# Latent attention on row tiles: first keys, values and gate tiles placed between the first row maxima, the transposed scores regrouped, and the first output tile's split moved

## The chip, the core and the metric

The kernel runs on one core of one Trainium2 chip. The metric is device time in microseconds (us) of one execution. Before the change the median of 3 runs is 1684.32 us (1684.28 to 1687.16). The core's engines each have a queue of their own: PE (TensorE, matrix products into PSUM), ACT (ScalarE), DVE (VectorE), POOL (GpSimd) and SP (SyncE, which only issues transfers). PSUM has eight banks of 128 x 512 fp32.

## The reference

Two layers over 1024 latent tokens and 256 context tokens of width 1024, in fp32: layer 0 is windowed attention, layer 1 is latent attention, and a final RMSNorm follows. The change touches only layer 1's attention and its output projection:

```python
def attend(qn, qr, kn, kr, v):
    s = (jnp.einsum("bqhd,bkhd->bhqk", qn, kn)
         + jnp.einsum("bqhd,bkd->bhqk", qr, kr)).astype(F32) * scale
    p = jax.nn.softmax(s, axis=-1).astype(v.dtype)
    return jnp.einsum("bhqk,bkhd->bqhd", p, v)
...
yx = (ox * jax.nn.silu(gx)) @ w_out
...
x = x + gate_x[:, None] * yx
...
return rms_norm(x, final_g)
```

There are 16 heads with 64 + 32 query and key columns and 64 value columns. 1024 queries see 1280 keys. Queries, keys (from a rank-256 latent) and the gate `g` come from projections that run before.

## The kernel before

Layer 0, the projections of layer 1 and the query tiles run first, until about 1009 us. From line 1389 on the code stands in a block in which the order of the instructions on PE, ACT and DVE is written by hand; SP's and POOL's queues are ordered by the framework, which also lets a few matmuls of the second output tile slip in at the block's end.

**Precision.** Most products are made of two-part numbers (a rounded high part and the rest). `split` (lines 118 to 121) makes the parts: ACT copies the high part (L120), another engine subtracts (L121). `mm3` (L125 to L127) is high*high, low*high, high*low.

**Units.** Attention runs in 32 units: head pair `i // 4`, head `e` in the pair, half of 512 queries. One unit has these steps, written out of order around those of its neighbours:

- `prep` loads the queries by SP.
- `top(b)`, b = 0 to 3, finds a row maximum for 128 queries: four matmuls 64x512 (L1161, two at a time on the two halves of PE's rows) and two of 64x256 on one half (L1164) fill `psm` (banks 0 to 2), then DVE reduces 1280 columns to one (L1166). The next `top` writes the same banks, so it waits for that reduction.
- `shift` transposes the maxima (L1170, into a corner of bank 2), DVE spreads them (L1171), ACT copies them (L1176). They enter the scores as extra rows of the product.
- `score(i, a, b)`, i = 0 to 4, makes transposed scores, 256 keys by 512 queries, in passes a to b of five; a pass is a pair of matmuls (L1192), one on each half of the rows. Scores alternate between two pairs of banks, `slots`. `expo(i)` is the exponential on ACT (L1198) that empties the pair; POOL then adds up the denominators (L1202, L1206). `hold=True` leaves `expo` to be called later.
- `PV` multiplies with the values (L1214, 20 matmuls, bank 7), `fin` and `fin1` put the halves together (ACT L1229, DVE L1233), `fin2` and `fin3` transpose and apply denominators and gate (PE L1243 and L1258, DVE L1244, L1247, L1259, ACT L1252, POOL L1261) and store to `og_d`.

In the loop over `ui` (lines 1415 to 1472) unit `ui` has its scores made while unit `ui - 1` has its `PV` and `fin` steps, unit `ui + 2` its `top(0)` and `top(1)`, unit `ui + 1` its `top(2)`, `top(3)` and `shift`. `make_K` makes a pair's keys in two calls (with `ui % 4` 0 and 1), ACT casting (L1125) and DVE subtracting (L1123); `make_V` makes the values of four heads (`ui % 8 == 0`, L1098).

**Start.** Ahead of the loop stand the rotary keys (`make_kr`), the first keys and values, the last gate tiles (`g_tile`, 24 matmuls 128x256 a half, SiLU on ACT at L994) and the first unit's `top` calls. With the first unit's scores stand `top(1)` to `top(3)` of unit 1, `make_K(1, (0, 2))` and `top(0)`, `top(1)` of unit 2.

**Output.** `out_tiles` (line 1286) is a generator that handles eight tiles of 128 rows: fetch, split, 48 products for two banks of columns, gate and residual (L1346, L1347), squares (L1348), norm, store. For the first tile seven of eight column blocks are fetched early; block 7 needs unit 30's `fin3` to be stored first. `next(out_fill)` runs it to the next `yield`. `wo_pieces` splits the output weights in the same way.

Of the kernel before, what the change touches and what calls it, by code (L numbers as in the profile page):

```python
# [59 lines left out]
def kernel(ctx: ExitStack, tc: tile.TileContext, t, out, dbg=None):  # L60
    nc = tc.nc
# [979 lines left out]
    NU = 32  # L1041
# [7 lines left out]
    accr = Ring(F, [47, 49], 512)  # L1049
    glr = Ring(R, [60, 62], 512)  # L1050
    otr = Ring(F, [0, 4], 1024)
    rbr = Ring(F, [8, 9], 256)
# [6 lines left out]
    def slot():  # L1059
        slots.reverse()  # L1060
        return slots[1]
# [224 lines left out]
    def out_tiles():  # L1286
        load2(out=gx1, in_=gate_d[1, 0, :].partition_broadcast(128))

# [8 lines left out]
        yield  # L1297
        load(out=fg, in_=t["final_g"].partition_broadcast(128))
        for ti in range(8):
# [5 lines left out]
            n = 7 if ti == 0 else 8  # L1305
            split(og[:, 0, 0:n], og[:, 1, 0:n], of[:, 0:n])
            st = sm_ring()
            css = [slice(c * 512, c * 512 + 512) for c in range(2)]
# [80 lines left out]
    with tc.manual_schedule(engines={E.PE, E.Activation, E.DVE}):  # L1389
# [10 lines left out]
        g_tile(9, 3, 1)  # L1400
        next(vk)
        next(vk)
        u0.top(0)
        next(vk)
        u0.top(1)
        g_tile(8, 4, 0, slots[0][:, 0])
        g_tile(8, 4, 1)
# [3 lines left out]
        u0.top(3)  # L1411
        g_tile(9, 4, 1)
        u1.top(0)
        u0.shift()
        for ui, u in enumerate(units):
            pu, ppu = [units[ui - n] if ui >= n else None for n in (1, 2)]
            nu, nnu = [units[ui + n] if ui + n < NU else None for n in (1, 2)]
            if nnu and ui:
                nnu.prep()
            u.score(0, 0, 1)  # L1420
            if ui == 0:
                u.score(0, 1, 4)
                nu.top(1)
                u.score(0, 4, 5)
                u.score(1, 0, 3)
                nu.top(2)
                u.score(1, 3, 5, hold=True)
                nu.top(3)
            else:
                if nu:  # L1430
                    nu.top(2)
                u.score(0, 1, 5)
                u.score(1, 0, 4)
                if nu:
                    nu.top(3)
                u.score(1, 4, 5, hold=True)
            x = slot()
            if ui % 4 == 0 and u.pair < 7:
                make_K(u.pair + 1, (0, 2), x)
            if ui % 4 == 1 and u.pair < 7:  # L1440
                make_K(u.pair + 1, (1,), x)
            if ui == NU - 1:
                next(out_fill)
            if pu:
                pu.PV()
            u.expo(1)
            if ui % 4 > 1 and ui < 23 or ui > 25:
                next(wo_fill)
            if pu:
                pu.fin()  # L1450
            if nu:
                nu.shift()
            if ppu and ppu.e == 1:
                ppu.fin3(x[:, 0])
            if pu:
                pu.fin2(x[:, 1])
            if ui and ui % 8 == 0:
                pu.fin1()
                for _ in make_V(u.pair // 2, x):
                    pass  # L1460
            if ui == NU - 1:
                next(out_fill)
            if nnu:
                nnu.top(0)
            if ui % 8:
                pu.fin1()
            u.score(2)
            u.score(3, 0, 3)
            if nnu:
                nnu.top(1)  # L1470
            u.score(3, 3, 5)
            u.score(4)
# [6 lines left out]
        u.fin1()  # L1479
        next(out_fill)  # L1480
        u.fin2(slot()[:, 0])
        next(out_fill)
        u.fin3(slot()[:, 0])
# [75 lines left out]
```

## Time and profile before

| | us |
|---|---|
| profiled execution | 1683.97 |
| its span (first to last instruction) | 1682.1 |
| median of 3 runs | 1684.32 |
| PE busy | 1581.9 (94%) |
| DVE busy | 1023.7 (61%) |
| ACT busy | 796.9 (47%) |
| POOL busy | 802.0 (48%) |
| granted PE clock, mean | 0.977 |

The profile shows one execution; its times count from the span's start. PE's matmuls overlap, so a busy PE need not be PE at its peak; PEld is the load of a matmul's stationary operand. What stands in brackets at a row's end is the engine's idle time before that row and what ended it. Units 1 to 30 lie between 1081 and 1549 us, about 14.3 us each, 16.7 with a `make_K` and 23.5 with a `make_V`.

### The profile page before, as it was taken

Reading aid. Unit: us, or ns where it says so; the run is one execution under the profiler, and the core shown is the slowest. Engines: PE = TensorE matmul, PEld = TensorE weight load, DVE = VectorE, ACT = ScalarE, POOL = GpSimd, SP = SyncE. Lnnn points to the kernel's source line nnn. Section 1 sums busy time; section 2 is a strip of 40 time slices with the busy share of each in tenths; the row PEclk is TensorE's granted clock in tenths of the full one; section 3 lists DMA queues with packets and bytes.
Section 4 is the critical chain, followed back from the end, with each engine's and each line's share of the span. In section 5 each row is a group of like instructions: output and inputs, shape, how many; then the busy total and the mean of one; then the engine's idle time right before and its main releaser. Section 6 shows DMA issues by size and latency. Waiting matters only on the chain.

```text
span 1682.1 us, 26928 instructions
## 1 busy us (share of the span) xinstructions
PE 1581.9 (94%) x9738; PEld 1238.9 (74%) x9738; DVE 1023.7 (61%) x2047; ACT 796.9 (47%) x1541; POOL 802.0 (48%) x774
## 2 busy tenths in 40 slices
PE   6899739999999999998999999899999999999898
PEld 2787628888788888887998999566766666766587
DVE  7898773327888888878534102566566566566254
ACT  3621112237877777777423312454454544544321
POOL 2556552222544333344324410478677677678300
PEclk9999869999999999999999999999999999999899
DMA  8455565145433333326117632213233232233151
GB/s 308 140 169 166 147 175 163 50 150 161 118 107 101 92 88 88 89 63 219 38 51 236 223 112 73 66 36 93 62 91 93 68 90 77 64 122 100 55 171 65
DMA packets 145476, 192.68 MB, mean 115 GB/s; under 512 B 14256, under 2 KB 82480, under 8 KB 145344
## 3 DMA queue, kind: packets, MB, share of 16 engines
q1 hardware_dynamic: 143584, 188.41, 37.5%
q10 hardware_dynamic: 1760, 2.56, 0.5%
q8 instruction: 76, 1.25, 0.3%
q14 instruction: 56, 0.46, 0.1%
HBM read 144.77 MB, written 46.15 MB: 114 GB/s over the span
## 4 chain that ended last, share of the span: by engine, by line
PE 46%; DVE 3%; ACT 2%; issue 1%; DMA 1%; POOL 1%; ACTq 0%; POOLq 0%; DVEq 0%; SPq 0%
PE PB L1192 11%; PE PB L1214 8%; PE PB L125 7%; PE PB L127 7%; PE PB L126 7%; PE PB L1161 4%; ACT arena_f L1198 1%; PE PB L1164 1%; PE PB L1243 1%; DVE arena_f L1166 1%; PE PB L1170 0%; DVE arena_r L121 0%; DMA arena_f<-b_w_in 0%; DMA x_d<-arena_f 0%; PE PB L1258 0%
## 5 line engine op out<-in xcount | busy, mean ns | idle before, releaser
L125 PE MATMUL PB<-arena_r 128*128 128x512 f32 (+2 forms) x1496 | 511.5, 343 | 25.5 <-DVE arena_f L445 13.2
L126 PE MATMUL PB<-arena_r 128*128 128x512 f32 (+2 forms) x1496 | 506.7, 339 | 5.2 <-DVE arena_r L280 2.6
L127 PE MATMUL PB<-arena_r 128*128 128x512 f32 (+2 forms) x1496 | 504.1, 337 | 0.6 <-DVE arena_r L121 0.6
L1206 POOL TENSOR_TENSOR arena_f<-arena_f 128x512 f32<-128x512 f32 x252 | 328.7, 1304 | 127.3 <-ACT arena_f L1198 111.1
L125 PEld LDWEIGHTS PB<-arena_r 128*128 128x128 f32 x1496 | 287.0, 192 | 62.9 <-DVE arena_f L445 14.6
L126 PEld LDWEIGHTS PB<-arena_r 128*128 128x128 f32 x1496 | 287.4, 192 | 35.6 <-DVE arena_r L280 4.5
L127 PEld LDWEIGHTS PB<-arena_r 128*128 128x128 f32 x1496 | 287.0, 192 | 29.7 <-DVE arena_r L121 1.2
L1166 DVE TENSOR_REDUCE arena_f<-PB 128x1 f32<-128x1280 f32 x128 | 190.2, 1486 | 130.2 <-PE PB L1164 124.3
L1192 PE MATMUL PB<-arena_r 64*128 64x512 f32 (+1 forms) x1600 | 244.6, 398 | 2.0
L1198 ACT ACTIVATE arena_f<-PB 128x1024 f32<-128x1024 f32 x160 | 164.1, 1026 | 139.8 <-PE PB L1192 92.5
L121 POOL TENSOR_TENSOR arena_r<-arena_f,arena_r 128x512 fp32r<-128x512 f32 x98 | 139.2, 1435 | 183.7 <-ACT arena_r L120 139.2
L1192 PEld LDWEIGHTS PB<-arena_r 64*128 64x128 f32 (+1 forms) x1600 | 179.0, 186 | 40.6 <-ACT arena_f L1198 16.4
L552 DVE CUSTOM_DVE_ANT_0 arena_f<-PB,arena_f,small 128x256 f32<-128x256 f32 (+1 forms) x288 | 145.6, 522 | 28.1 <-PE PB L546 22.0
L121 DVE TENSOR_TENSOR arena_r<-PB,arena_r 128x512 fp32r<-128x512 f32 (+1 forms) x198 | 128.4, 657 | 27.6 <-ACT arena_r L120 27.0
L1214 PE MATMUL PB<-arena_f 128*64 128x512 f32 x640 | 144.4, 597 | 0.0
L194 DVE SCALAR_TENSOR_TENSOR arena_f<-arena_f,small 128x512 f32<-128x512 f32 x126 | 124.5, 1032 | 22.5 <-DMA arena_f<-ada_w 22.0
L555 ACT ACTIVATE arena_f<-arena_f,small 128x640 f32<-128x640 f32 (+2 forms) x160 | 119.3, 747 | 28.6 <-DVE small L554 27.8
L120 ACT CAST arena_r<-PB 128x512 fp32r<-128x512 f32 (+1 forms) x198 | 108.9, 561 | 49.3 <-PE PB L573 27.1
L583 PE MATMUL PB<-arena_r 128*128 128x512 f32 x336 | 123.3, 441 | 4.3 <-ACT arena_f L594 3.2
L120 ACT CAST arena_r<-arena_f 128x512 fp32r<-128x512 f32 (+2 forms) x146 | 87.1, 610 | 83.6 <-DVE arena_f L455 18.5
L573 PE MATMUL PB<-ident,arena_f 128*128 128x128 f32 x672 | 110.6, 274 | 1.3 <-ACT arena_f L555 1.1
L1214 PEld LDWEIGHTS PB<-arena_f 128*64 128x64 f32 x640 | 43.1, 137 | 81.4 <-issue 80.2
(157 smaller groups left out, 2082.0 us busy)
## 6 DMA issues: line engine op xcount, KB each, us to landing
arena_f<-ada_w SPq DMA_DIRECT2D x82, 256.0 KB, 3.6
arena_r<-q_d SPq DMA_DIRECT2D x80, 256.0 KB, 3.9
arena_r<-qn_d SPq DMA_DIRECT2D x64, 256.0 KB, 3.8
arena_r<-qr_d SPq DMA_DIRECT2D x192, 64.0 KB, 3.1
arena_f<-a_w_in SPq DMA_DIRECT2D x40, 256.0 KB, 3.2
q_d<-arena_f SPq DMA_DIRECT2D x80, 128.0 KB, 2.4
g_d<-arena_f SPq DMA_DIRECT2D x36, 256.0 KB, 2.9
arena_f<-x SPq DMA_DIRECT2D x16, 512.0 KB, 4.5
```

The source lines that it names most:

```text
L120: nc.scalar.copy(hi, src)
L121: (lo_eng or nc.vector).tensor_sub(lo, src, hi.bitcast(F32))
L125: nc.tensor.matmul(o, ah, bh, start=first, stop=False)
L126: nc.tensor.matmul(o, al, bh, start=False, stop=False)
L127: nc.tensor.matmul(o, ah, bl, start=False, stop=last)
L194: nc.vector.scalar_tensor_tensor(accs[i], w, sc[:, k, i : i + 1], accs[i], ALU.mult, ALU.add)
L552: nc.vector.tensor_tensor_reduce(o, S, mk, 1.0, prev, ALU.add, ALU.max, mx)
L1166: nc.vector.reduce_max(self.mx[:, 32 + b : 33 + b], flat, AX.X, negate=True)
L1192: nc.tensor.matmul(S[:, t], k[r, c : c + 128], q[r], start=j == 0, stop=j == 4)
L1198: nc.scalar.activation(E, self.S, AF.Exp)
L1206: eng.tensor_add(self.acc, self.acc, E[:, t])
L1214: nc.tensor.matmul(self.pv[p : p + 64], Vq[:, cs[t], self.h % 4, :], E[:, t], start=i == 0, stop=i == 4)
```

## The change

No product is added or dropped. One tiny activation is new (`warm`, one column through the exponential), and the load of the gate row `gx1` goes from ACT's queue to SP's. The rest is order:

```diff
 def out_tiles():
-    load2(out=gx1, in_=gate_d[1, 0, :].partition_broadcast(128))
+    load(out=gx1, in_=gate_d[1, 0, :].partition_broadcast(128))
...
     nxt = fetch(0, 7)
     yield
-    load(out=fg, in_=t["final_g"].partition_broadcast(128))
...
         split(og[:, 0, 0:n], og[:, 1, 0:n], of[:, 0:n])
+        if ti == 0:
+            yield
+            load(out=fg, in_=t["final_g"].partition_broadcast(128))
...
-    next(vk)
-    next(vk)
+    for _ in vk:
+        pass
     u0.top(0)
-    next(vk)
+    g_tile(8, 4, 0, slots[0][:, 0])
     u0.top(1)
-    g_tile(8, 4, 0, slots[0][:, 0])
     g_tile(8, 4, 1)
...
     g_tile(9, 4, 1)
+    nc.scalar.activation(warm, const[:, 1:2], AF.Exp)
+    u0.shift()
     u1.top(0)
-    u0.shift()
+    make_K(1, (0, 2), slots[1])
+    u1.top(1)
     for ui, u in enumerate(units):
...
-        u.score(0, 0, 1)
         if ui == 0:
-            u.score(0, 1, 4)
-            nu.top(1)
-            u.score(0, 4, 5)
+            u.score(0)
             u.score(1, 0, 3)
             nu.top(2)
             u.score(1, 3, 5, hold=True)
+            x = slot()
+            make_K(1, (1,), x)
             nu.top(3)
+            u.expo(1)
+            u.score(2)
+            nu.shift()
         else:
+            u.score(0, 0, 2)
             if nu:
                 nu.top(2)
-            u.score(0, 1, 5)
+            u.score(0, 2, 5)
...
+            if ui == NU - 2:
+                next(out_fill)
             pu.PV()
             u.expo(1)
...
+            if ui == NU - 1:
+                next(out_fill)
             pu.fin()
...
         if nnu:
             nnu.top(0)
...
-        u.score(2)
-        u.score(3, 0, 3)
+        if ui:
+            u.score(2)
+        u.score(3)
         if nnu:
             nnu.top(1)
-        u.score(3, 3, 5)
         u.score(4)
     pu.fin3(slot()[:, 0])
     next(out_fill)
     next(out_fill)
     u.PV()
     u.fin()
     u.fin1()
     next(out_fill)
+    next(out_fill)
     u.fin2(slot()[:, 0])
+    next(out_fill)
     next(out_fill)
     u.fin3(slot()[:, 0])
```

The `next(out_fill)` now at `NU - 2` stood at `NU - 1`, and the one now ahead of `pu.fin()` stood behind `pu.fin2`. Of the calls ahead of `PV` the loop's `make_K` lines stay, except that the call with block 1 for pair 1 is the one shown at `ui == 0`. The new lines move the numbers of the changed kernel's helper lines up by one: L1166 is L1167 there, and so on; in `out_tiles` by three.

PE in the loop, one unit before, from `fin2` (L1243) of the unit behind to `top(3)`: L1161 and L1164 are a `top`, L1192 the matmuls of `score`.

```order
L1243 MATMUL PB<-ident,arena_f 128x128 x4
L1161 MATMUL PB<-arena_r 128x512 x4
L1164 MATMUL PB<-arena_r 128x256 x2
L1192 MATMUL PB<-arena_r 128x512 x16
L1161 MATMUL PB<-arena_r 128x512 x4
L1164 MATMUL PB<-arena_r 128x256 x2
L1192 MATMUL PB<-arena_r 128x512 x16
L1161 MATMUL PB<-arena_r 128x512 x4
```

The same unit now:

```order
L1244 MATMUL PB<-ident,arena_f 128x128 x4
L1162 MATMUL PB<-arena_r 128x512 x4
L1165 MATMUL PB<-arena_r 128x256 x2
L1193 MATMUL PB<-arena_r 128x512 x20
L1162 MATMUL PB<-arena_r 128x512 x4
L1165 MATMUL PB<-arena_r 128x256 x2
L1193 MATMUL PB<-arena_r 128x512 x14
L1162 MATMUL PB<-arena_r 128x512 x4
```

Between `top(0)` and `top(1)` there were 16 matmuls and are 20; between `top(1)` and `top(2)`, and again between `top(2)` and `top(3)`, there were 16 and are 14.

DVE at the start, before: L1166 reduces for `top`, L1171 is `shift`, L1123 the subtractions of `make_K`.

```order
L1166 TENSOR_REDUCE arena_f<-PB 128x1 x5
L1171 TENSOR_TENSOR arena_r<-PB,ident 4x512
L1166 TENSOR_REDUCE arena_f<-PB 128x1 x3
L1123 TENSOR_TENSOR arena_r<-PB,arena_r 64x512 x2
L1123 TENSOR_TENSOR arena_r<-PB,arena_r 64x256 x4
L1171 TENSOR_TENSOR arena_r<-PB,ident 4x512
```

And now:

```order
L1167 TENSOR_REDUCE arena_f<-PB 128x1 x4
L1172 TENSOR_TENSOR arena_r<-PB,ident 4x512
L1167 TENSOR_REDUCE arena_f<-PB 128x1
L1124 TENSOR_TENSOR arena_r<-PB,arena_r 64x512 x2
L1124 TENSOR_TENSOR arena_r<-PB,arena_r 64x256 x4
L1167 TENSOR_REDUCE arena_f<-PB 128x1 x2
L1124 TENSOR_TENSOR arena_r<-PB,arena_r 64x512 x2
L1167 TENSOR_REDUCE arena_f<-PB 128x1
L1172 TENSOR_TENSOR arena_r<-PB,ident 4x512
```

The first unit's `shift` now stands ahead of unit 1's first reduction, and the six subtractions stand ahead of the reductions for unit 1's `top(1)` to `top(3)` where they stood behind them.

ACT in the last unit, before: L1198 is `expo`, L120 128x512 the split of a weight piece, L120 128x896 the split of the first output tile, L1229 `fin`, L1252 `fin2`.

```order
L1198 ACTIVATE arena_f<-PB 128x1024 x4
L1287 DMA arena_f<-gate_d 128x1024
L1198 ACTIVATE arena_f<-PB 128x1024
L120 CAST arena_r<-arena_f 128x512
L1229 COPY arena_f<-PB 64x512
L1252 COPY arena_f<-small 128x256 x2
L120 CAST arena_r<-arena_r 128x896
L1198 ACTIVATE arena_f<-PB 128x1024 x3
```

And now:

```order
L1199 ACTIVATE arena_f<-PB 128x1024 x5
L120 CAST arena_r<-arena_f 128x512
L120 CAST arena_r<-arena_r 128x896
L1230 COPY arena_f<-PB 64x512
L1253 COPY arena_f<-small 128x256 x2
L1199 ACTIVATE arena_f<-PB 128x1024 x3
```

The first output tile's split comes ahead of `fin` instead of behind `fin2`. On PE the twelve products of it that stood ahead of the last unit's scores 2 to 4 now stand behind them.

40 lines of the change are left out of this document (17 added, 23 removed).

## The prediction

> **What bounds the kernel now.** I read the page's slices first (PE busy nearly everywhere), then the table of stages, then the waits of PE's loads, then the timeline at the three places that the change touches. The table of stages has, behind each stretch, its length and PE's busy time:
>
> ```profile
> 1080.86:1548.99 468.13, 465.84 (x3216) 302.08 (x3215) 283.79 (x295) 233.25 (x304) 353.75 (x274) 1.00 0.28 80
> 1601.00:1664.30 63.30, 63.30 (x281) 52.40 (x280) 33.35 (x45) 15.64 (x32) 6.16 (x18) 1.00 0.39 129
> ```
>
> In the loop and in the output stage PE never stands still for long; DVE (284 of 468 us), ACT and POOL have slack. So only PE's small waits count. In the loop these are, by the waits of the load queue (1081 to 1549 us):
>
> ```profile
> PEld PB L1192 <- ACT arena_f L1198: 14.4, 29, 0.5
> PEld PB L1161 <- DVE arena_f L1166: 12.9, 56, 0.6
> ```
>
> Once in each of 29 units a score waits for an exponential to empty its banks, and about twice a `top` waits for the reduction before it. One unit's timeline shows where (T0 to T3 are the four L1161 rows):
>
> ```profile
> 1232.05 0.73 PE L1161 MATMUL PB<-arena_r 64*128 64x512 f32 x4
> ...
> 1232.85 2.03 PE L1192 MATMUL PB<-arena_r 64*128 64x512 f32 x15
> ...
> 1234.61 0.74 PE L1161 MATMUL PB<-arena_r 64*128 64x512 f32 x4
> ...
> 1235.62 1.49 DVE L1166 TENSOR_REDUCE arena_f<-PB 128x1 f32<-128x1280 f32 x1 [0.35 <-PE PB L1164]
> 1236.22 2.13 ACT L1198 ACTIVATE arena_f<-PB 128x1024 f32<-128x1024 f32 x2 [0.89 <-PE PB L1192]
> ...
> 1237.30 0.19 PEld L1192 LDWEIGHTS PB<-arena_r 64*128 64x128 f32 x2 [0.52 <-ACT arena_f L1198]
> ...
> 1237.64 0.63 PE L1161 MATMUL PB<-arena_r 64*128 64x512 f32 x4
> ...
> 1238.53 1.49 DVE L1166 TENSOR_REDUCE arena_f<-PB 128x1 f32<-128x1280 f32 x1 [1.42 <-PE PB L1164]
> ...
> 1240.08 0.74 PE L1161 MATMUL PB<-arena_r 64*128 64x512 f32 x4
> ```
>
> T1 (1234.61) waits for T0's reduction. The ACT row holds `expo(3)` and `expo(4)`: the first ends near 1237.25, and the next unit's `score(0)` starts at 1237.30, after 0.5 us. T3 comes 0.06 us behind the end of T2's reduction (1238.53 + 1.49 = 1240.02).
>
> **The loop, part by part.** No work goes; PE's order changes. A pair of L1192 costs 0.234 us: 15 matmuls in 2.03 us, the last of them 0.4 us long, so 1.63/14 for one. `score(3)` is now whole before `top(1)`, so T1 follows T0 by ten pairs instead of eight: 0.80 (1232.85 less 1232.05) + 10 x 0.234 = 3.14 us on that half of PE's rows that did `top(0)`'s short matmuls, one pair earlier, 2.9, on the other. T0's reduction is over at 2.5, so T1 no longer waits. `expo(3)` starts when `expo(2)` is done, near 3.3, ends near 4.4, and PE reaches `score(0)` at 3.14 + 0.46 (its share of `top(1)`, two pairs) + 5 x 0.234 = 4.8: the 0.5 us wait goes.
>
> What is late next is DVE's chain. From T2 to T3 the rows show 0.89 + 1.49 + 0.06 = 2.44 us if the first `top` did not wait; from T1, which waited, its reduction starts 1.01 later (1235.62), which makes 2.56. PE now has only seven pairs between T1 and T2 and between T2 and T3. T2 can come at 2.9 + 2.44 = 5.34, while PE is there at 3.14 + 0.46 + 7 x 0.234 = 5.24; T3 at 5.34 + 2.56 = 7.90. Today T3 is 8.03 behind T0. `PV` follows T3 as before. So a plain unit gains 0.13 us, little beside the 0.9 us of waits, because the reductions take most of it. Other kinds of units have more DVE work behind T0 (the multiplication L1259, a reciprocal), which T1 waits out today and no longer will:
>
> ```profile
> 1217.60 0.73 PE L1161 MATMUL PB<-arena_r 64*128 64x512 f32 x4
> ...
> 1225.79 0.73 PE L1161 MATMUL PB<-arena_r 64*128 64x512 f32 x4
> ...
> 1246.35 0.73 PE L1161 MATMUL PB<-arena_r 64*128 64x512 f32 x4
> ...
> 1254.51 0.73 PE L1161 MATMUL PB<-arena_r 64*128 64x512 f32 x4
> ...
> 1263.48 0.73 PE L1161 MATMUL PB<-arena_r 64*128 64x512 f32 x4
> ...
> 1271.78 0.73 PE L1161 MATMUL PB<-arena_r 64*128 64x512 f32 x4
> ```
>
> These are T0 and T3 of loop turns with `ui % 4` of 1, 3 and 0: 8.19, 8.16 and 8.30. Against 7.90 they gain 0.29, 0.26 and 0.40. Of the 29 turns from 1 to 29, 11 count as plain (remainder 2, turn 1, and the three with `make_V`, which I take to be like them), 7, 7 and 4 are of these kinds: 11 x 0.13 + 7 x 0.29 + 7 x 0.26 + 4 x 0.40 = **6.9 us**. Bounds: 0, if a waiting `top` costs 0.12 us more per link than I take, up to 10, if T2 starts as cheaply as an unwaited one (29 x 0.12 more).
>
> **The start.** The gate halves between the `top` calls and the values made at once cost nothing: PE has 24 matmuls of 0.12 us (2.9 us) between two `top` calls, more than the 2.44 of a reduction, so the last gate half ends at 1051.25 as now. From there:
>
> ```profile
> 1051.25 0.73 PE L1161 MATMUL PB<-arena_r 64*128 64x512 f32 x4
> ...
> 1053.80 0.32 PE L1170 MATMUL PB<-ident,arena_f 128*100 128x128 f32 x1 [1.58 <-DVE arena_f L1166]
> ...
> 1064.18 2.70 ACT L1125 CAST arena_r<-PB 64x512 fp32r<-64x512 f32 x6 [6.35 <-PE PB L127]
> ...
> 1065.38 3.25 DVE L1123 TENSOR_TENSOR arena_r<-PB,arena_r 64x512 fp32r<-64x512 f32 x6 [2.22 <-ACT arena_r L1125]
> ...
> 1069.40 0.38 PE L1164 MATMUL PB<-arena_r 64*128 64x256 f32 x1 [3.77 <-DVE arena_r L1171]
> ...
> 1075.71 0.64 PE L1161 MATMUL PB<-arena_r 64*128 64x512 f32 x4
> ...
> 1080.86 4.51 PE L1214 MATMUL PB<-arena_f 128*64 128x512 f32 x20
> ```
>
> Today `shift` waits 1.58 us for unit 1's `top(0)`, and unit 2's `top(0)` waits 3.77 for a `shift` product queued behind six subtractions. Now `shift` goes first at 1051.25 and frees bank 2 about 1.05 later, `make_K` runs 1052.7 to 1054.9 on PE, the six casts 1054.2 to 1057.0, the six subtractions, 1.2 behind the casts' start, 1055.4 to 1058.7. The waits are not gone but moved: `score(1)` needs the banks that the subtractions read, so PE stands from 1056.6 (after `score(0)`) to 1058.7; `top(2)` needs a reduction that is now queued behind them, 1058.7 + 1.5 = 1060.3. On at half clock for one window, as today: `make_K(1, (1,))` ends at 1064.7, `top(3)` at 1065.3. `expo(1)` is queued on ACT behind two casts and `score(2)` needs its banks: 1067.1. `shift` waits for a reduction behind two subtractions: 1069.0; then DVE's spread, one `top`, a reduction: unit 2's `top(1)` at 1072.2, unit 1's `top(2)` at 1074.8 where it stands at 1075.71, `PV` at 1078.4 (no `make_K` before it) instead of 1080.86. Gain **2.4 us**. `warm` takes the table load off ACT while ACT idles. Bounds: 0.5 (one more half-clock window, about 1.7 us of work lost) and 4.5 (none).
>
> The clock by the table of stages (its third figure from the right):
>
> ```profile
> 1056.76:1060.17 3.41, 1.64 (x13) 1.02 (x13) 2.19 (x2) 1.05 (x2) 1.27 (x1) 1.00 0.92 227
> 1060.17:1063.58 3.41, 3.41 (x11) 2.61 (x12) 1.49 (x1) 0.00 (x0) 0.00 (x0) 0.50 0.86 228
> ```
>
> A window with 1.64 us of matmuls in 3.41 was followed by one at half clock. The changed start has about 0.9 us in that window, so I keep one half-clock window in the sum. [...]
>
> **The end.** Today, after unit 30's `PV`:
>
> ```profile
> 1565.51 0.66 PE L1243 MATMUL PB<-ident,arena_f 128*128 128x128 f32 x4 [0.25 <-POOL arena_f L1206]
> ...
> 1567.16 0.71 ACT L1252 COPY arena_f<-small 128x256 f32<-128x256 f32 x2 [1.28 <-DVE small L1247]
> 1567.78 0.93 ACT L120 CAST arena_r<-arena_r 128x896 fp32r<-128x896 f32 x1
> 1568.74 1.57 DVE L121 TENSOR_TENSOR arena_r<-arena_r 128x896 fp32r<-128x896 f32 x1 [1.61 <-ACT arena_r L120]
> ...
> 1570.37 0.80 PE L126 MATMUL PB<-arena_r 128*128 128x512 f32 x1 [0.81 <-DVE arena_r L121]
> ...
> 1575.36 4.18 PE L1192 MATMUL PB<-arena_r 64*128 64x512 f32 x30
> ...
> 1580.87 2.94 DVE L1206 TENSOR_TENSOR arena_f<-arena_f 128x512 f32<-128x512 f32 x4 [9.83 <-POOL arena_f L1206]
> ...
> 1584.61 1.28 POOL L1261 TENSOR_TENSOR arena_f<-arena_f,arena_r 128x512 f32<-128x512 f32 x1 [3.77 <-DVE arena_f L1259]
> ...
> 1593.15 1.04 ACT L120 CAST arena_r<-arena_r 128x1024 fp32r<-128x1024 f32 x1 [3.17 <-DMA arena_r<-og_d]
> 1594.23 1.23 DVE L121 TENSOR_TENSOR arena_r<-arena_r 128x1024 fp32r<-128x1024 f32 x1 [3.52 <-ACT arena_r L120]
> ...
> 1599.96 0.60 PE L1258 MATMUL PB<-ident,arena_f 128*128 128x128 f32 x4
> ```
>
> PE stands from 1566.2 to 1570.4 for the first tile's split, then runs twelve products at half clock, and only at 1575.36 come the last unit's scores, from which everything later hangs: exponentials, sums, `fin3` of unit 30 (which DVE does behind the last unit's sums), its store and the fetch (1584.61 + 1.28 to 1593.15: 7.3 us), the second tile's split, `fin2`. Now the split is on ACT at 1563.6 and DVE until 1566.2, in idle time there, and PE goes on at 1566.0 with the 30 score matmuls. ACT's L1252 still ends at 1567.9, so the three exponentials end at 1568.9, 1569.9 and 1571.5, and `score(4)` waits 0.65 us: scores until 1570.1, `fin3`'s transposes until 1570.6, 21 products until 1575.4, `PV` (4.5) until 1579.9, 21 products until 1584.7, `fin2` until 1585.3. Beside it the sums: POOL until 1572.0, DVE's four (2.94) until 1575.0, L1259 and L1261 until 1577.0, plus 7.3 for store and fetch 1584.3: ACT's split until 1585.4, DVE's until 1586.6, on which PE waits 1.3 us. Nine products more, then `fin2`'s results and the last block's split near 1588.9, six products, `fin3` at 1590.3. Today `fin3` is at 1599.96 with three products fewer ahead of it (0.7 us): gain **10.3 us**, and the output stage, all PE, starts that much earlier. No gap here is over 1.3 us, so no half clock. Bounds: 5 (the store and fetch take 5 us longer, or the split holds ACT's queue) to 11. The load of `gx1` on SP is behind a store it needs; what stands behind it on SP is needed microseconds later, so I cost it at nothing, up to 0.5 us if a weight piece comes late.
>
> Sum: 6.9 + 2.4 + 10.3 = 19.6. The profiled execution took 1683.97 (span 1682.1), 0.35 under the median: 1683.97 - 19.6 = 1664.4.
>
> **The rivals.** *The reductions eat the loop's gain* (0.17): each waiting `top` costs some 0.1 more and T3 stays as far behind T0 as today: 1664.4 + 6.9 = 1671.3. For it: two waiting links in a row, where today one is free; against: T1's wait and the score's wait are really gone. *The start loses* (0.10): two more half-clock windows, 1664.4 + 3.4 = 1667.8. For it: 1.8 us of work between 1063.6 and 1067. *The change does not do what it says at the end* (0.08): the split is early, but the stage still hangs on the store and fetch of block 7, gain 5: 1669.7. For it: the 7.3 us are untouched. *Slower* (0.05): in the loop L1233 stands on DVE between the reductions of T0 and T1; if it or what is before it slips past the moment T1's matmuls are done (3.9 us behind T0), T1's reduction, T2 and T3 slip in each of 29 turns. Break-even is a slip of 0.68 us a turn (19.6/29); at 0.8 the time would be 1664.4 + 23.2 = 1687.6. Against: by the rows the addition ends near 3.2 to 3.6.
>
> **How the numbers follow.** The forecast, 0.60: 1664.4. The range 1660 to 1673 goes down to the loop's and the start's better bounds together in part (4.4 us) and up to the first three rivals with 1.7 us to spare. What can be told from no change is 0.2%, 3.4 us: faster 0.91, same 0.04, slower 0.05.
>
> **What would show it.** In the changed profile: no wait of L1193 for ACT in the loop; T0 to T3 of 7.9 in all kinds; waits of L1162 for DVE at T2 and T3, none at T1; first `PV` near 1078.4; the scores of the last unit right behind `fin2`; no half clock after 1549 until the last few us. Wrong it is if T0 to T3 stays at 8.03 or more, or if PE still stands for over 2 us between 1549 and 1590.

## The result, and the profile after

| | median us | all | executions |
|---|---|---|---|
| before | 1685.53 | 1684.28 to 1687.16 | 4 |
| after | 1671.18 | 1665.15 to 1673.27 | 4 |
| after, again | 1666.14 | 1662.33 to 1670.53 | 5 |

The change is faster: the ratio after to before is 0.9908 (95% interval 0.988 to 0.9937), and 0.9897 (0.9881 to 0.9913) the second time. The profiled execution took 1665.15 us (span 1663.4) where 1664.4 was forecast. The median of all nine is 1668.7; why they spread over 11 us, where 17 executions of before in the second session lie within 5.5, is a question of its own below.

I cut the span at three marks: the first matmul of the rotary keys (L1068, now L1069), the first `PV` (L1214, now L1215), the last `PV` but one, and the last unit's `fin3`. The table of stages for PE alone gives for each stretch its length, PE's busy time and the granted clock. Before:

```profile
1011.11:1080.86 69.75, 61.89 (x445) 0.95 0.27 78
1080.86:1560.75 479.89, 477.57 (x3292) 1.00 0.28 79
1560.75:1599.96 39.21, 32.56 (x140) 0.87 0.22 68
```

After:

```profile
1011.59:1077.47 65.88, 60.65 (x445) 1.00 0.29 83
1077.47:1551.16 473.69, 473.65 (x3292) 1.00 0.30 81
1551.16:1581.93 30.77, 28.56 (x143) 1.00 0.21 64
```

Start 3.9, loop 6.2, end 8.4 us less, and the output stage behind it (82.14 and 81.47 us) 0.7 less; the part ahead of the first mark took 0.5 more. That makes the 18.7 us between the two spans.

**The loop.** In the waits of the load queue (1077.5 to 1539.4 us) the wait of the scores for an exponential is gone, and the wait for reductions has grown from 12.9 us:

```profile
PEld PB L1162 <- DVE arena_f L1167: 23.1, 58, 0.4
```

One plain turn on PE's timeline:

```profile
1226.88 0.74 PE L1162 MATMUL PB<-arena_r 64*128 64x512 f32 x4
...
1229.76 0.40 PE L1162 MATMUL PB<-arena_r 64*128 64x512 f32 x1
...
1232.24 0.73 PE L1162 MATMUL PB<-arena_r 64*128 64x512 f32 x4
...
1234.78 0.73 PE L1162 MATMUL PB<-arena_r 64*128 64x512 f32 x4
...
1235.92 1.08 PE L1215 MATMUL PB<-arena_f 128*64 128x512 f32 x4
```

T1, T2 and T3 stand 2.88, 5.36 and 7.90 behind T0. T1 waits for nothing; T2 and T3 come when DVE has reduced, as its timeline shows:

```profile
1227.89 1.49 DVE L1167 TENSOR_REDUCE arena_f<-PB 128x1 f32<-128x1280 f32 x1
1229.41 0.68 DVE L1234 TENSOR_TENSOR arena_f<-PB,arena_f 64x512 f32<-64x512 f32 x1
1230.69 1.49 DVE L1167 TENSOR_REDUCE arena_f<-PB 128x1 f32<-128x1280 f32 x1 [0.59 <-PE PB L1165]
1233.24 1.49 DVE L1167 TENSOR_REDUCE arena_f<-PB 128x1 f32<-128x1280 f32 x1 [1.05 <-PE PB L1165]
```

The second reduction ends at 1232.18 and T2 is at 1232.24; the third at 1234.73, T3 at 1234.78. The other kinds of turn, T0 and T3 of the same turns as the prediction's (remainder 1, then 0; for remainder 3 the two stand at 1241.04 and 1248.97):

```profile
1212.75 0.73 PE L1162 MATMUL PB<-arena_r 64*128 64x512 f32 x4
...
1220.64 0.73 PE L1162 MATMUL PB<-arena_r 64*128 64x512 f32 x4
...
1257.96 0.73 PE L1162 MATMUL PB<-arena_r 64*128 64x512 f32 x4
...
1265.96 0.73 PE L1162 MATMUL PB<-arena_r 64*128 64x512 f32 x4
```

7.89 us for remainder 1, 7.93 for 3 and 8.00 for 0, where they were 8.19, 8.16 and 8.30.

**The start.** PE's timeline shows the waits at the places that were named, and in this execution no half clock:

```profile
1059.33 0.96 PE L1193 MATMUL PB<-arena_r 64*128 64x512 f32 x5 [1.38 <-DVE arena_r L1124]
1060.86 0.73 PE L1162 MATMUL PB<-arena_r 64*128 64x512 f32 x4 [0.56 <-DVE arena_f L1167]
...
1066.17 1.42 PE L1193 MATMUL PB<-arena_r 64*128 64x512 f32 x10 [1.42 <-ACT arena_f L1199]
```

**The end.** The timeline behind unit 30's `PV` (all engines):

```profile
1554.88 1.93 DVE L121 TENSOR_TENSOR arena_r<-arena_r 128x896 fp32r<-128x896 f32 x1
...
1555.83 2.14 POOL L1203 TENSOR_TENSOR arena_f<-arena_f 128x512 f32<-128x512 f32 x1
...
1555.92 0.66 PE L1244 MATMUL PB<-ident,arena_f 128*128 128x128 f32 x4 [0.25 <-POOL arena_f L1207]
...
1556.51 2.60 PE L1193 MATMUL PB<-arena_r 64*128 64x512 f32 x20
...
1558.05 5.40 POOL L1207 TENSOR_TENSOR arena_f<-arena_f 128x512 f32<-128x512 f32 x4
...
1563.48 2.94 DVE L1207 TENSOR_TENSOR arena_f<-arena_f 128x512 f32<-128x512 f32 x4 [5.11 <-POOL arena_f L1207]
...
1566.45 0.69 DVE L1260 TENSOR_TENSOR arena_f<-arena_f,PB 128x512 f32<-128x512 f32 x1
1567.22 1.28 POOL L1262 TENSOR_TENSOR arena_f<-arena_f,arena_r 128x512 f32<-128x512 f32 x1 [3.77 <-DVE arena_f L1260]
...
1575.45 0.60 PE L1244 MATMUL PB<-ident,arena_f 128*128 128x128 f32 x4
1575.88 1.04 ACT L120 CAST arena_r<-arena_r 128x1024 fp32r<-128x1024 f32 x1 [4.64 <-DMA arena_r<-og_d]
...
1576.98 0.49 PE L125 MATMUL PB<-arena_r 128*128 128x512 f32 x1 [0.93 <-ACT arena_r L120]
1578.24 0.50 PE L126 MATMUL PB<-arena_r 128*128 128x512 f32 x1 [0.77 <-DVE arena_r L121]
```

The scores stand right behind `fin2`; the stand of 4.2 us for the first tile's split is gone. What is left are 1.7 us (0.93 and 0.77) in which PE waits for the second tile's split, and that waits for the store and fetch of block 7: 7.38 us from the end of L1262 (1568.50) to the cast (1575.88), where it was 7.26 before.

POOL's addition L1203 takes 2.14 us here, while DVE subtracts for the first tile's split (L121). Before, that split came later, and the same addition of the last unit took 1.27:

```profile
1565.41 1.27 POOL L1202 TENSOR_TENSOR arena_f<-arena_f 128x512 f32<-128x512 f32 x1
```

### The profile page after: what moved, and what is told of

It is laid out like the page before. It is cut to its first block, busy times and chain, and to the rows that moved or that the text cites. A ratio compares the mean times of both kernels' runs of the same rounds, so it can differ in the third digit from the quotient of the medians.

```text
span 1663.4 us, 26928 instructions
## 1 busy us (share of the span) xinstructions
PE 1571.5 (94%) x9738; PEld 1234.5 (74%) x9738; DVE 1029.6 (62%) x2047; ACT 797.4 (48%) x1542; POOL 805.7 (48%) x774
## 3 DMA queue, kind: packets, MB, share of 16 engines
q10 hardware_dynamic: 1616, 2.04, 0.4%
## 4 chain that ended last, share of the span: by engine, by line
PE 66%; DVE 6%; ACT 4%; issue 2%; DMA 2%; POOL 1%; SPq 0%; DVEq 0%; POOLq 0%; ACTq 0%
PE PB L1193 11%; PE PB L125 10%; PE PB L127 10%; PE PB L126 10%; PE PB L1215 8%; PE PB L1162 5%; PE PB L583 3%; PE PB L573 3%; DVE arena_r L121 2%; PE PB L545 2%; PE PB L546 1%; DVE arena_f L552 1%; ACT arena_f L555 1%; PE PB L1165 1%; PE PB L1244 1%
## 5 line engine op out<-in xcount | busy, mean ns | idle before, releaser
L1207 POOL TENSOR_TENSOR arena_f<-arena_f 128x512 f32<-128x512 f32 x252 | 329.0, 1306 | 107.9 <-ACT arena_f L1199 91.7
L1167 DVE TENSOR_REDUCE arena_f<-PB 128x1 f32<-128x1280 f32 x128 | 190.3, 1487 | 117.8 <-PE PB L1165 109.0
L1193 PE MATMUL PB<-arena_r 64*128 64x512 f32 (+1 forms) x1600 | 230.0, 392 | 3.1 <-ACT arena_f L1199 1.7
L121 POOL TENSOR_TENSOR arena_r<-arena_f,arena_r 128x512 fp32r<-128x512 f32 x98 | 140.5, 1447 | 181.0 <-ACT arena_r L120 138.4
L1193 PEld LDWEIGHTS PB<-arena_r 64*128 64x128 f32 (+1 forms) x1600 | 175.1, 185 | 28.5 <-ACT arena_f L1199 3.4
L121 DVE TENSOR_TENSOR arena_r<-PB,arena_r 128x512 fp32r<-128x512 f32 (+1 forms) x198 | 128.6, 658 | 27.7 <-ACT arena_r L120 27.0
L1215 PE MATMUL PB<-arena_f 128*64 128x512 f32 x640 | 144.4, 597 | 0.0
L120 ACT CAST arena_r<-PB 128x512 fp32r<-128x512 f32 (+1 forms) x198 | 109.0, 561 | 49.0 <-PE PB L573 29.6
L120 ACT CAST arena_r<-arena_f 128x512 fp32r<-128x512 f32 (+2 forms) x146 | 87.2, 610 | 86.6 <-DVE arena_f L455 18.4
L1215 PEld LDWEIGHTS PB<-arena_f 128*64 128x64 f32 x640 | 43.1, 136 | 81.2 <-issue 80.1
```

What stands on the lines that cost most here:

```text
L120: nc.scalar.copy(hi, src)
L121: (lo_eng or nc.vector).tensor_sub(lo, src, hi.bitcast(F32))
L1167: nc.vector.reduce_max(self.mx[:, 32 + b : 33 + b], flat, AX.X, negate=True)
L1193: nc.tensor.matmul(S[:, t], k[r, c : c + 128], q[r], start=j == 0, stop=j == 4)
L1207: eng.tensor_add(self.acc, self.acc, E[:, t])
L1215: nc.tensor.matmul(self.pv[p : p + 64], Vq[:, cs[t], self.h % 4, :], E[:, t], start=i == 0, stop=i == 4)
```

## The experiments

My theory: the change is three independent gains. In the loop all of it comes from `score(3)` being whole before `top(1)`; DVE's chain of reductions then sets T2 and T3. The start's gain depends on the clock. At the end the split's stand goes. The rivals: the reductions eat the loop's gain; the start loses; the end hangs on block 7 anyway.

**One part at a time.** The kernel before with the loop's regrouping alone (turns 1 to 31):

```diff
-            u.score(0, 0, 1)
...
+                u.score(0, 0, 2)
                 if nu:
                     nu.top(2)
-                u.score(0, 1, 5)
+                u.score(0, 2, 5)
...
-            u.score(3, 0, 3)
+            u.score(3, 0, 5 if ui else 3)
             if nnu:
                 nnu.top(1)
-            u.score(3, 3, 5)
+            if ui == 0:
+                u.score(3, 3, 5)
```

> The kernel before with the loop's regrouping alone (two score pairs before top(2), score(3) whole before top(1), for turns 1 to 31). My theory: T0 to T3 falls to 7.9 us in all kinds of turn, no L1192 waits for ACT, and the time falls by about 6.9 us (the changed kernel's profile, which has the same loop, gave 6.2 from the first PV to that of turn 30). Rival, the reductions eat the gain: T0 to T3 stays at 8.03 and the time falls by under 1.5 us. Rival, slower: over 1690.

1675.85 us median of 6, ratio 0.9962 (0.9949 to 0.9975), that is 6.4 us (8.2 between the medians); the loop by the table of stages:

```profile
1079.85:1553.65 473.80, 473.77 (x3292) 1.00 0.29 80
```

6.1 us less than before, as in the changed kernel (473.69). The reductions did not eat it.

The start alone (the lines ahead of the loop and the branch for `ui == 0`):

```diff
+        u0.shift()
         u1.top(0)
-        u0.shift()
+        make_K(1, (0, 2), slots[1])
+        u1.top(1)
...
```

> The kernel before with the changed start alone (all that stands ahead of the loop and the turn with ui of 0). My theory: the first loop PV comes 2.4 to 3.8 us earlier than the 1080.86 of before, and the time falls by as much. Rival, the start loses: half-clock windows in the start's stands (PE stands 1.4 to 2.2 us four times) take it back, the time falls by 0 to 1 us or rises, and the trace has two windows at 0.50 between 1052 and 1082.

1682.07 us median of 11, ratio 0.999 (0.9981 to 0.9998): 1.7 us, of which the interval leaves 0.3 to 3.2, so the times alone do not decide between theory and rival. In the trace the stretch of the start takes 66.82 us, 2.9 less than before, with one window at half clock. (The first `PV` itself stands at 1081.04, because the part ahead of the start was 3.1 us longer in this execution.)

The end alone:

```diff
-            if ui == NU - 1:
+            if ui == NU - 2:
                 next(out_fill)
             if pu:
...
+            if ui == NU - 1:
+                next(out_fill)
             if pu:
                 pu.fin()
...
-            if ui == NU - 1:
-                next(out_fill)
...
```

> The kernel before with the changed end alone (the first output tile's split ahead of fin, its twelve products behind the last unit's scores, the gate row's load on SP). My theory: fin3 of the last unit comes 9 to 10 us earlier behind PV of turn 30 than before, and the time falls by 10.3 us. Rival, the stage still hangs on the store and fetch of block 7: it falls by 5 us or less, and the PE rows show a wait for the fetched block of several us.

1676.94 us median of 6, ratio 0.9963 (0.9951 to 0.9975): 6.2 us (7.1 between the medians), between the theory and the rival. The last stretch takes 32.60 us, 6.6 less than before, where 9 to 10 were expected, and 1.8 more than in the changed kernel. PE waits 2.04 us for the second tile's split, where the changed kernel's trace has 0.93 + 0.77, and the window behind that wait is at half clock:

```profile
1585.06:1588.47 3.41, 1.53 (x5) 1.00 0.00 0
1588.47:1591.89 3.42, 3.42 (x10) 0.50 0.74 212
```

The three ratios together make 14.3 us of 1684; the whole change made 15.5 and 17.3 by its two ratios. The parts add up within what the intervals leave open.

**The spread.** The changed kernel once more:

> The changed kernel once more, for the spread of its times: its profiled execution took 1665.15 and the other three 1670.4 to 1673.3. Theory A: windows at half clock, whose phase differs from execution to execution, fall into the stands of the new start or of the end in most executions; then a second trace whose time is near 1671 has two or more windows at half clock (about 1.7 us each) that the first trace has not, and a mean granted clock of 0.976 to 0.979 where that one had 0.983. Theory B: something else (a transfer that lands late) makes them longer; then the windows are the same and one wait of PE is longer by several us. Time 1671 median.

1666.14 us median of 5, where 1671 was expected; the profiled one took 1668.70. Theory A holds as far as the clock goes, but only one of the additional windows lies in the start; the rest lie ahead of the block. Its three stretches, against those of the first trace:

```profile
1014.28:1081.12 66.84, 62.15 (x444) 0.97 0.29 82
1081.12:1554.84 473.72, 473.65 (x3292) 1.00 0.30 81
1554.84:1585.47 30.63, 28.55 (x142) 1.00 0.21 65
```

Loop and end are the same to 0.2 us. The start is 1.0 longer, and ahead of it 2.7 us were lost: by the clock's own record 64.9 us are at half clock there where the first trace has 54.6, three windows more (the mean granted clock is 0.978 against 0.983). The half clock of the start comes from one window. In the first trace every step of the clock's record lies on a grid of 3.41 us: its stretches at half clock are 3.41, 6.83 and 30.72 us long, but for the last, which ends with the trace. The table of stages, cut at this grid, for the first trace:

```profile
1055.77:1059.18 3.41, 2.19 (x17) 1.00 0.84 223
1059.18:1062.59 3.41, 2.70 (x17) 1.00 0.86 224
```

and for the second, whose work is 2.7 us later there, so that the window lies 0.4 us later in it:

```profile
1058.82:1062.23 3.41, 2.04 (x17) 1.00 0.87 221
1062.23:1065.65 3.42, 3.38 (x15) 0.50 0.89 222
```

The same wait of `score(1)`, cut 0.4 us differently, leaves 2.19 or 2.04 us of matmuls in a window, and the next runs at full or half clock. Over the nine traces that have the changed start (these two, e2, and the runs e5 to e8, e11 and e12, which follow below) there were 0, 0, 1, 1, 2, 2, 3, 3 and 3 such windows in the stretch:

| windows at half clock | stretch, us |
|---|---|
| 0 | 65.88, 65.90 |
| 1 | 66.82, 66.84 |
| 2 | 68.22, 68.25 |
| 3 | 68.40, 68.48, 68.75 |

(The 68.40 and 68.48 are of e7 and e11, whose first `PV` has one pair less ahead of it, 0.23 us.) The three traces with the start of before have two windows each: 69.21, 69.75, 69.77. So the start's gain lies between 1 and 3.9 us by the window's place. The end's lies between 6.6 and 9.1 against the 39.21 of before (which holds half clock too; e1 and e2 have 38.06 and 38.48 there); three of the seven traces with that end, e3, e5 and e7, have a window at half clock in it. The part ahead differs by 5 us between traces for the same reason: the first mark stands at 1009.50 with 47.8 us at half clock ahead of it, at 1014.65 with 64.9, and in between for what lies between. These three ranges add up to between 10 and 11 us, nearly the whole spread; that the slowest and the fastest execution had them all at once is not shown, since they left no trace.

**What carries the loop.** Three changes of where the tops stand, with the pairs between them. Two take back one half of the regrouping each:

```diff
-                u.score(0, 0, 2)
+                u.score(0, 0, 1)
                 if nu:
                     nu.top(2)
-                u.score(0, 2, 5)
+                u.score(0, 1, 5)
```

> The changed kernel with top(2) back after one pair of score(0), so that 10, 6 and 8 pairs stand between its tops instead of 10, 7 and 7. My theory: T1 to T2 and T2 to T3 are set by DVE's reductions (2.47 and 2.54 us), not by PE; T2 and T3 stay where they are, T0 to T3 stays at 7.9, and from the first PV to that of the last unit but one it takes 473.7 us as in the changed kernel. All of the loop's gain then comes from score(3) being whole before top(1). Rival, PE's pairs count: the longer third link costs 0.23 us a turn, some 480 us.

```diff
-            u.score(3)
+            u.score(3, 0, 3 if ui else 5)
             if nnu:
                 nnu.top(1)
+            if ui:
+                u.score(3, 3, 5)
```

> The changed kernel with top(1) back between the third and fourth pass of score(3), so that 8, 9 and 7 pairs stand between the tops. My theory: expo(3) is late again, score(0) waits some 0.5 us for it, one pair more than in the kernel before stands behind that wait before T2, and the third link stays at DVE's 2.47; T0 to T3 becomes 8.2 to 8.3 us and the loop 484 to 487 us where the kernel before has 479.9 and the changed one 473.7. Rival, moving top(2) helps by itself: under 479 us.

One execution each, 1672.28 and 1677.92 us. The loop of the first, and of the second:

```profile
1082.90:1556.83 473.93, 467.83 (x3292) 1.00 0.30 81
```

```profile
1078.19:1564.60 486.41, 484.19 (x3291) 1.00 0.29 79
```

473.9 and 486.4, as the theory had it: `top(2)` behind one pair or two is all the same, since T2 and T3 wait for DVE either way, and moving it alone would have cost 6.5 us against before. The waits of the second's load queue (1085 to 1530 us) show why, in 27 turns:

```profile
PEld PB L1193 <- ACT arena_f L1199: 13.3, 27, 0.5
```

The third uses the idle time that the reductions leave PE ahead of T3:

```diff
-                u.score(1, 0, 4)
+                u.score(1, hold=True)
                 if nu:
                     nu.top(3)
-                u.score(1, 4, 5, hold=True)
```

> The changed kernel with top(3) behind the whole of score(1) instead of ahead of its last pair. My theory: PE is idle 0.3 us ahead of T3 because it waits for the reduction of T2, so the pair (0.234 us) fits in there, and T3 stays at 7.9 behind T0 while PV follows it without that pair: 29 x 0.234 = 6.8 us less, loop 466.9 us. Rival: the pair behind top(3) covers a wait of PV, or T3 moves by as much: no gain, 473.7 us.

1661.11 us median of 4, ratio 0.9858 (0.9838 to 0.9878). The loop, and a turn's T2, T3 and `PV`:

```profile
1077.90:1544.94 467.04, 466.96 (x3291) 1.00 0.30 82
```

```profile
1230.60 0.73 PE L1162 MATMUL PB<-arena_r 64*128 64x512 f32 x4
...
1233.15 0.74 PE L1162 MATMUL PB<-arena_r 64*128 64x512 f32 x4
1234.04 4.51 PE L1215 MATMUL PB<-arena_f 128*64 128x512 f32 x20
```

6.65 us less than the changed kernel, where 6.8 were expected. From T2 to T3 it is 2.55 us, as with one pair less (2.54), and `PV` follows T3 by 0.89 instead of 1.14. PE had room there because DVE is the limit.

**The end's second wait.** Unit 30's `fin3` goes ahead of the last unit's `score(4)`, so that L1260 is not queued on DVE behind sums that wait for POOL:

```diff
-            u.score(3)
+            if ui == NU - 1:
+                u.score(3, hold=True)
+                pu.fin3(slot()[:, 0])
+                u.expo(3)
+                next(out_fill)
+            else:
+                u.score(3)
...
-        pu.fin3(slot()[:, 0])
-        next(out_fill)
```

> The changed kernel with fin3 of the last unit but one moved ahead of the last unit's score(4) and of DVE's four sums, with twelve of the products between. My theory: in the changed kernel L1260 waits on DVE behind sums that themselves wait for POOL (idle 5.1 us), and so the store and fetch of block 7 and the second tile's split come late and PE stands 1.7 us; now the store starts when POOL has done its sums, some 3.8 us earlier, that stand is gone, and the last unit's fin3 comes 1.7 us earlier behind its PV's predecessor: 29.0 instead of 30.7 us. Rival: score(4) coming 2 to 3 us later delays POOL's and DVE's last sums and fin2, and nothing is gained.

```profile
1562.72 0.69 DVE L1260 TENSOR_TENSOR arena_f<-arena_f,PB 128x512 f32<-128x512 f32 x1 [1.75 <-PE PB L1259]
...
1565.99 1.28 POOL L1262 TENSOR_TENSOR arena_f<-arena_f,arena_r 128x512 f32<-128x512 f32 x1
...
1573.73 1.05 ACT L120 CAST arena_r<-arena_r 128x1024 fp32r<-128x1024 f32 x1 [5.83 <-DMA arena_r<-og_d]
...
1578.29 0.60 PE L1244 MATMUL PB<-ident,arena_f 128*128 128x128 f32 x4
```

The cast is 4.6 us ahead of `fin2` where it was 0.4 behind, PE no longer waits, and `fin3` stands 28.88 us behind the last `PV` but one (29.0 expected, 30.77 in the changed kernel). The time, 1666.64 us median of 4, ratio 0.9895 (0.987 to 0.992), cannot be told from the changed kernel's; this trace has three windows at half clock in its start. So the mechanism is shown, its worth in time is not. Both edits together:

> The changed kernel with both edits of the runs before, top(3) behind the whole of score(1) and fin3 ahead of the last unit's score(4). My theory: the gains add, loop 467.0 us and fin3 28.9 us behind the last PV but one, time 6.7 + 1.8 to 3.5 us under the changed kernel's 1666 to 1671 median, 1659 us. Rival: the fin3 edit's gain is lost to noise of the start, 1661 us like the run with top(3) alone.

1660.51 us median of 4, ratio 0.9853 (0.9836 to 0.9869), loop 466.98, end 28.88: the stretches add. The time does not show it: it is 1.5 over the expectation and within 0.6 of the run with `top(3)` alone, which is what the rival said. The profiled execution, with three windows at half clock in its start, took 1658.52.

**The activation `warm`.** Its one line taken out:

```diff
-        nc.scalar.activation(warm, const[:, 1:2], AF.Exp)
```

> The changed kernel without the tiny activation of the start. My theory: the table load of 1.3 us comes with the first exponential instead, which PE waits for only behind pair 1's keys; score(2) and first PV come no later than by 0.5 us: stretch to the first PV within the 73.3 to 76.2 us of the traces of the changed start. Rival: the load delays the first casts and all behind them by 1.3 us: a stretch of 74.6 us or more without half clock.

1664.60 us, one execution; stretch to the first `PV` 65.90 us without half clock, 65.88 with the line. It brings nothing that shows. The table load is a row of ACT, 1.28 us long, which stands at 1055.50 with the first exponential before and at 1052.52 with `warm` now.

**The start without stands.** On top of both edits, the key steps split so that DVE's part can stand elsewhere:

```diff
         u0.top(1)
-        g_tile(8, 4, 1)
+        sK = steps_K(1, (0, 2), slots[1])
+        next(sK)
         units[2].prep()
         u0.top(2)
...
+        for _ in sK:
+            pass
+        g_tile(8, 4, 1)
         u0.top(3)
...
         u0.shift()
         u1.top(0)
-        make_K(1, (0, 2), slots[1])
+        g_tile(9, 4, 1)
...
+                sK = steps_K(1, (1,), PB[:, 7:8, :]) if ui == 1 else iter(())
+                next(sK, None)
                 u.score(0, 0, 2)
                 if nu:
                     nu.top(2)
+                for _ in sK:
+                    pass
...
```

`steps_K` is `make_K` with a `yield` between its products and its casts. Here `units[2].prep()` loads queries over the weights of gate block 8 before their last use. So this kernel does not compute the gate of the last 256 rows, though it runs the same instructions; it stands here for its times.

> The changed kernel with top(3) behind score(1) and fin3 moved as in the two runs before, and with the start ordered anew so that PE has work at each wait for DVE: pair 1's first keys made between the first unit's top(1) and top(2) with their subtractions queued behind top(2)'s reduction, the last gate half between unit 1's top(0) and top(1), the keys' block 1 in the bank of PV between unit 2's top(1) and top(2). My theory: the start's loss is PE standing 1.4 us and more in a window of the clock, which grants half clock in the next; without the stands no window between the first top and the first PV is at half clock and the stretch of 73.3 to 76.2 us in the changed start becomes 69.6 us, every time. Time about 5 us under the kernel without this (e11_both), 1655 us. Rival: the extra work on DVE between reductions, and the keys in PV's bank, delay the tops by as much: 73 us or more, no gain.

The stretch took 64.90 us, 3.6 less than in the run with both edits, and the median of 4 fell to 1655.08 us, ratio 0.9822 (0.9803 to 0.984). (The marks of the expectation begin 7.4 us earlier, at a product ahead of the rotary keys: 69.6 there is 62.2 here.) But one window of the clock was at half, behind one in which PE stood 1.58 us ahead of unit 2's `top(1)`, since I had left `score(4)` behind both tops:

```profile
1065.13:1068.55 3.42, 1.73 (x11) 1.00 0.71 186
1068.55:1071.96 3.41, 3.41 (x17) 0.51 0.00 0
```

So the last run moves it:

```diff
-        units[2].prep()
         u0.top(2)
...
         g_tile(8, 4, 1)
+        units[2].prep()
...
             if ui == 0:
-                pass
+                u.score(4)
...
-            u.score(4)
+            if ui:
+                u.score(4)
```

> The kernel of e10_start2 with two moves: unit 2's queries are loaded behind the last use of the weights of gate block 8, whose place in memory they take (in e10_start2 they took it before, so the gate of the last 256 rows had other values there, from the same instructions), and score(4) of the first unit stands between unit 2's top(0) and top(1) instead of behind both. My theory: the stand of 1.58 us ahead of unit 2's top(1), and with it the half-clock window of 3.4 us that followed it, go; the stretch to the first PV falls from the 72.3 us of e10_start2 to about 70 us with no window at half clock, and the time to 1653 us median where e10_start2 had 1655.1 and e11_both 1660.5. Rival: PE still stands as long elsewhere between the first PV's tops, the window at half clock is not due to that stand, and the stretch stays at 72 us.

```profile
1013.46:1075.66 62.20, 59.63 (x445) 1.00 0.31 88
```

62.20 us, which is the 69.6 of e10's expectation, and full clock throughout. 1655.35 us median of 5 (1654.20 to 1655.86), ratio to before 0.9832 (0.9818 to 0.9846): the best version here that computes all of the gate. Its five executions lie within 1.7 us. The stand and the window went as expected, the median did not fall to 1653: against e10's it gained nothing. Its own trace is 2.9 us shorter in span than e10's, but that one was the slowest of e10's four executions (1653.41 to 1658.66), and 1.1 us of the 2.9 lie at the end (28.88 against 30.01), which neither move touches; the cause of that 1.1 was not shown. The trace of e13 has 61.4 us at half clock ahead of the block, e10's 58.0. So the worth of the last two moves in time stays open.

## Why the prediction was right, point by point

*The loop (6.9 forecast, 6.2 measured).* T1 free, T2 at 5.34, T3 at 7.90: the rows show 2.88, 5.36 and 7.90. The two waits went, and the reductions took back most, as was said. Most of the miss is the turns with remainder 0: they were put at 7.90 and take 8.00. There DVE has both the multiplication and the reciprocal ahead of T0's reduction, which ends 2.84 us behind T0 (1259.36 + 1.44 less 1257.96), and T1 still follows it. The rival that the reductions eat the gain fell with e1. The rival of the slower side fell too: L1234 ends 3.21 us behind T0 (1229.41 + 0.68 less 1226.88) and DVE then idles 0.59 us before T1's reduction, so it has that much room.

*The start (2.4 forecast; 3.9, 2.9 or as little as 1.0 measured).* Each wait stands at the place that was worked out (the `top(2)` put at 1074.8 is unit 2's, not unit 1's), though the first is 1.38 us where 2.1 was put. But "I keep one half-clock window" was one draw of a lottery: the traces have none to three. The reason given for it was mis-sized too: 0.9 us of matmuls were put into the window that holds the wait of `score(1)`, and there are 2.19 or 2.04, a load that leads to full clock in one trace and to half in the other. The rival "the start loses" is what happened, by its windows, in three of nine traces; even there the stretch is 1.0 us shorter than before. For no such window 4.5 was named, and the first trace has 3.9. That the first profiled execution had none was luck: e4's, with the same wait cut 0.4 us differently, has one.

*The end (10.3 forecast; 9.1 measured, 8.4 and the output stage's 0.7).* Scores, products and `PV` came at the forecast places. The step that was mis-sized is "POOL until 1572.0": counted from unit 30's `PV` (1560.75, now 1551.16) that is 11.3 us, and it took 12.3 (1558.05 + 5.40 less 1551.16). POOL works from L1203 on without a pause, so the queue of its sums, not the exponentials, sets their end, and 0.87 us of the 1.0 is L1203 alone, 2.14 us beside DVE's subtraction where it was 1.27 before. The same addition takes 2.13 us in e4 and 2.14 in e3 and e8. So "the split is on ACT at 1563.6 and DVE until 1566.2, in idle time there" was right for those two engines and had no price for POOL. DVE's sums, L1260, the store, the fetch and the split are 1 us later each, and PE waits 1.7 instead of 1.3. "No gap here is over 1.3 us, so no half clock" failed with it: in three of seven traces a window at half clock follows, and the stretch is 1.5 to 2.0 us longer there. The prediction's own row spoke against it: the window with 1.64 us of work, which led to half clock, holds two stands of 0.65 and 1.11 us, neither over 1.3. The rival of a gain of 5 fell by the stretches, 6.6 less in e3 and 8.4 in the changed kernel; the interval of e3's ratio, 4.2 to 8.3 us, would not exclude it.

*The signs.* All that were named came but two: the turns with remainder 0 take 8.00, not 7.9, and in three later traces there was half clock at the end. "PE still stands for over 2 us between 1549 and 1590" was to show it wrong. The longest single stand there is 0.93 us; all small ones of the last stretch together come to 2.2 (30.77 less 28.56), so read as a sum this sign was just met.

*The time.* The sum met the profiled execution to 0.8 us (1665.15), in part by luck: a start 1.5 better than forecast, without half clock, made up for an end 1.2, a loop 0.7 and a part ahead 0.5 worse. The first median lies 6.8 above the forecast, the second 1.7; by e4 and the table of starts that distance is windows at half clock, in the start, at the end and ahead of the block. That is shown for the executions with a trace; for the others it is inferred from their mean clock, 0.976 to 0.979 in the four that took 1670.4 to 1673.3 us and 0.982 to 0.984 in the three that took 1662.3 to 1665.2.

## What to carry to other kernels

When two engines hand work to and fro, write down the chain of the slower one first: the gap between two dependent steps has a floor (here 2.47 to 2.55 us per reduction), and work moved into a gap below its floor is free (e7: the loop falls from 473.69 to 467.04 us), while work moved out of it saves nothing (e5: 473.93). The waits that went off PE here reappeared in part as the next links' waits (12.9 us of waits for reductions became 23.1), so follow the chain to the step that really ends. Work moved into an engine's idle time can still slow its neighbour: look at what runs beside it (L1203 at the end, 2.14 us beside DVE's subtraction where it was 1.27). Stands of 1.4 us were worth filling here: with them the start took 65.88 to 68.75 us in nine traces, with none to three windows of 3.41 us at half clock; in the trace of e13, which fills them, it took 62.20 us at full clock. One trace can show the lucky case, and the spread over executions tells more than the trace.

## What the runs showed of the hardware

In the traces of before and after, every step of the granted clock lies on a grid of 3.41 us. Cut at it, the two have 15 full-clock windows with under 1.5 us of PE work (0 to 1.48), all followed by half clock; 17 with 1.5 to 2.3 us, of which two, with 1.64 and 1.83, were followed by half clock and the others, one of them with 1.54, by full; and 76 with 2.3 to 3.2 us, none followed by half clock. Of the later traces' windows shown above, 1.53 us (e3), 1.73 (e10) and 2.04 (e4) were followed by half clock. From half clock, the 22 windows with under 2.6 us of work were followed by half clock again, the 15 with 3.07 to 3.41 by full. By the table of starts a window at half clock lengthened the start by 0.4 to 1.4 us. That is less than it added to PE's busy time (60.65 us with none in the first trace, 64.71 with three in e8's), because PE's idle time in the stretch shrank meanwhile, from 5.23 to 4.04 us. At the end it added some 1.45 us of PE's busy time (28.56 and 30.01 in the changed kernel and e3).

POOL's additions and DVE's subtraction L121, both between tiles of `arena_f` and `arena_r`, each took longer where the other was already running. In the same two traces the 504 additions of L1203 and L1207 (the numbers of the changed kernel) with no L121 of DVE beside them took 1.26 to 1.30 us. Of the 64 beside one, the 31 that had begun before the subtraction took 1.26 to 1.29, and the 33 that began after it, while it ran, took 1.59 to 2.14. The subtraction of a weight piece (128x512) took 1.07 to 1.50 us in the 30 cases in which an addition was running when it began. At the end it begins 0.01 us (before) or 0.03 us (after) ahead of an addition: there DVE takes 0.69 us and POOL 1.81 or 1.79.
